# An encoder trunk on one core: the way from the output projection into the channel mixer, with the third tile turned inside the last projection and some sums on GpSimd

## The chip, the core and the metric

The kernel runs on one core of a Trainium2 chip. Its engines are TensorE (PE, with its weight loads as PEld), VectorE (DVE), ScalarE (ACT), GpSimd (POOL) and SyncE (SP), which issues most of the DMAs. Each engine works through its own list of instructions in a fixed order and waits on semaphores for the others. The metric is the device time of one execution in microseconds (us); lower is better.

## What is computed

Two requests, of 256 and 512 rows of width 1024 in f32, go through two layers with the same parameters. Each layer is a token mixer followed by a SwiGLU channel mixer, both between two RMS norms and added to the residual.

```python
def trunk(x, ...):
    for i in range(DEPTH):                          # 2 layers
        h = rms_norm(x, norm_mix_pre[i])
        m = window_gqa_sink(h, ...) if i % 2 == 0 else diff_attention(h, ...)   # end in "o @ w_o"
        x = x + rms_norm(m, norm_mix_post[i])
        h = rms_norm(x, norm_ffn_pre[i])
        x = x + rms_norm(swiglu(h, ffn_w_gate_up[i], ffn_w_down[i]), norm_ffn_post[i])
    return x

def swiglu(h, w_gate_up, w_down):
    g, u = jnp.split(h @ w_gate_up, 2, axis=-1)
    return (jax.nn.silu(g) * u) @ w_down
```

## The kernel before

The 768 rows are six tiles of 128, tiles 0 to 2 and 3 to 5. Every matrix product is made from three products of fp32r operands: a value is split into a high part (`hi`, a cast on ACT) and a low part (`lo`, value minus `hi`, on DVE), and hi·hi, hi·lo and lo·hi are added in PSUM (`product_steps`). The weights come from DRAM by SP's queue into a few buffers (`wraw`, `y_wraw`), are split by `two_parts` into `whi` and `wlo`, and a buffer's next load is issued once its low part has been made. `prepare` and `free` set how far this runs ahead.

The products of the channel mixer are made by a scheme that saves one of eight block products, on rows (tiles 0 to 2 against 3 to 5) and on halves of the columns. It needs combinations of both operands. For the activations, `combine` makes them: for a tile t < 3 it turns the tile on PE (`transpose`) and keeps `hhi`, `hlo` and a plain copy (`oa` in the first layer, `ob` in the second). For t >= 3 it turns the tile and makes s1, s2, s3 and a12 - s2 with the copy of tile t - 3, each split in two parts (`s1hi`, `s1lo` and so on). For the weights, `prepare` makes four combinations in place ("t32": L286 to L289, `b22` being split at L250 and L251), and the two pieces "t32" and "t14" are then split.

The stretch in question lies between the two, once in each layer. `project` multiplies the attention's result by the output weights; `staged` goes through the second half of the columns (`po_1`) in the order of tiles 0, 3, 1, 2, 4, 5, and between two half units of products it places the stages of the earlier tiles that `finish` returns: stage_a is 1/rms of the projection (`rstd_post`: an addition on ACT, a power on POOL), stage_b adds the residual (`x`), stores it and makes 1/rms of x (`rstd_pre`), stage_c scales x by it (`y_po`) and stage_d turns and combines it. The last five stages (two of tile 4, three of tile 5) are left over and become `later` in `ffn`, which places them among the first products of the channel mixer: p1 makes chunk c's px from a11 (tiles 0 to 2, left half) and copies it to `sv`, p2 adds the product with a12 and applies Silu (`ga`), p4 makes pz from a22, p6 and p5 make py and pw from s2 and s1. `u[0]` and `u[1]` are weight units of the first chunks.

The code's order is not yet the engines' order: a scheduler places each instruction when the kernel is built, by its dependences, by `high_priority` and by `issue_after`, which keeps the marked instructions behind another one. After that the order of each engine is fixed.

Of the kernel before, what the change touches and what calls it, by code (L numbers as in the profile page):

```python
# [17 lines left out]
P = 128  # L18
# [49 lines left out]
def trunk(  # L68
# [143 lines left out]
    ffn_units(1)  # L212

    raws, parts, b22s = {}, {}, {}
    state = {"dma": 0, "split": 0, "used": 0, "w": 0, "y": 0, "tt": 0, "rb": 0}
    tpool, dpool = [None], [None]
    quarters = {"tt": [], "rb": []}

# [29 lines left out]

    def two_parts(hi, lo, src):
        state["raw_hi"] = nc.scalar.copy(out=hi, in_=src)  # L250
        state["raw_lo"] = nc.vector.tensor_tensor(out=lo, in0=src, in1=hi.bitcast(F32), op=ALU.subtract)  # L251

    def prepare(upto):

# [75 lines left out]
    def split(hi, lo, src):  # L330
        state["hi"] = nc.scalar.copy(out=hi, in_=src)  # L331
        state["lo"] = nc.vector.tensor_tensor(out=lo, in0=src, in1=hi.bitcast(F32), op=ALU.subtract)  # L332

    def product_steps(out, pairs, start=True, stop=True, more=False):

        last = len(pairs) - 1

        def step(i):
            (ah, al), (bh, bl) = pairs[i]
            nc.tensor.matmul(out, ah, bh, start=start and i == 0, stop=False, skip_group_check=more)  # L343
            nc.tensor.matmul(out, ah, bl, start=False, stop=False, skip_group_check=more)  # L344
            nc.tensor.matmul(out, al, bh, start=False, stop=stop and i == last, skip_group_check=more)  # L345

        return [lambda i=i: step(i) for i in range(len(pairs))]

# [41 lines left out]

    def row_rstd(src, junk, name):
        ss = small.tile([P, 1], F32, tag="ss", name=f"ss_{name}")
        nc.scalar.activation(out=junk, in_=src, func=AF.Square, scale=D ** -0.5, accum_out=ss)
        return rstd(ss, eps_sb[:, 0:1], name)

    def scaled(y, src, r, g):
# [51 lines left out]
    def combine(src, t, name, comb, o):  # L448

        at = (t % 3) * P

        def turn(b):
            tp = bank(f"tp_{name}_{b}")
            for j in range(4):
                k = 4 * b + j  # L460
                nc.tensor.transpose(tp[:, j * P:(j + 1) * P], src[:, k * P:(k + 1) * P], ident)
            return tp

        v4 = lambda v: v.rearrange("p (k n) -> p k n", k=4)
        into = lambda half, b: tuple(v[half][:, 4 * b:4 * b + 4, at:at + P] for v in (h_hi, h_lo))
        if t < 3:
            for b in range(2):
                tp = turn(b)
                split(*into(0, b), v4(tp))
                nc.scalar.copy(out=o[t][:, b * 512:(b + 1) * 512], in_=tp)  # L470
            return
        a11, a12 = o[t - 3][:, :512], o[t - 3][:, 512:]
        s1, a22, s3, s2 = o[t][:, :512], o[t][:, 512:], src[:, :512], src[:, 512:]
        tp1, tp0 = turn(1), turn(0)
        nc.scalar.copy(out=a22, in_=tp1)
        split(*into(1, 1), v4(tp1))
        nc.vector.tensor_tensor(out=s1, in0=tp0, in1=a22, op=ALU.add)
        nc.vector.tensor_tensor(out=s3, in0=tp0, in1=a11, op=ALU.subtract)
        nc.vector.tensor_tensor(out=s2, in0=s1, in1=a11, op=ALU.subtract)
        split(*(v[:, :, at:at + P] for v in comb["s2"]), v4(s2))  # L480
        split(*into(1, 0), v4(s3))
        split(*(v[:, :, at:at + P] for v in comb["s1"]), v4(s1))
        nc.vector.tensor_tensor(out=a12, in0=a12, in1=s2, op=ALU.subtract)
        split(*(v[:, :, at:at + P] for v in comb["s4"]), v4(a12))

    def finish(sub, t, o, ssy, x, g, comb):

        r = {}
        m, (ss, y) = o[t], ssy

        def stage_a():
            with tc.high_priority():
                r[0] = rstd(ss[:, 1:2], ss[:, 0:1], f"post{sub}_{t}")

        def stage_b():
            with tc.high_priority():
                state["add"] = nc.vector.scalar_tensor_tensor(  # L500
                    out=x, in0=m, scalar=r[0], in1=x, op0=ALU.mult, op1=ALU.add)
                if g is not None:
                    r[1] = row_rstd(x, y, f"pre{sub + 1}_{t}")
            nc.sync.dma_start(out=x_at[sub + 1][t], in_=x)

        def stage_c():
            with tc.high_priority():
                scaled(y, x, r[1], g)

        def stage_d():  # L510
            if comb is not None:
                combine(y, t, f"h{sub + 1}_{t}", comb, o)
                return
            for s in transposes(y, t, f"h{sub + 1}_{t}"):
                s()

        return [stage_a, stage_b] + ([stage_c, stage_d] if g is not None else [])
# [9 lines left out]
    def staged(sub, units, o, sq, g, comb=None):  # L527

        st = []
        for i, t in enumerate((0, 3, 1, 2, 4, 5) if comb is not None else range(NT)):
            x = load_x(sub, t)
            units[t][0]()
            if i >= 2 and g is not None:
                st[i - 2][2]()
            if i >= 1:
                st[i - 1][1]()
            units[t][1]()  # L540
            if i >= 2 and g is not None:
                st[i - 2][3]()
            if g is None and t == NT - 1:
                last_tile(sub, t, o[t], sq[t], x, sq["last"])
                break
            st.append(finish(sub, t, o, sq[t], x, g, comb))
            st[i][0]()
        if g is None:
            return []
        return [st[NT - 2][2], st[NT - 1][1], st[NT - 2][3], st[NT - 1][2], st[NT - 1][3]]  # L550
# [18 lines left out]
    def out_unit(t, wk, o, n2, gp, sq, name):  # L569

        pm = bank(name)
        steps = product_steps(pm, [(htile(t, k), wk[k]) for k in range(KT)])
        if t == NT - 1:
            steps = releasing(steps, 4)
        return steps + [lambda: project_end(t, pm, o, n2, gp, sq, name)]

    def project_end(t, pm, o, n2, gp, sq, name):  # L580
            if n2 == 0:
# [443 lines left out]
    def ffn(layer, later, comb, cpool, cstack, ostack, gains):  # L1025
# [22 lines left out]
        def p1(c, unit):  # L1048
            mul(X, c, "px", "a11", unit, 0)
            sv[c] = temp("sv", c, AHEAD + 1, cpool)  # L1050
            nc.scalar.copy(out=sv[c], in_=X[c])

        def p2(c, unit):
            mul(X, c, "px", "a12", unit, 1, True)
            ga[c] = temp("ga", c, AHEAD + 1, cpool)
            nc.scalar.activation(out=ga[c], in_=X.pop(c), func=AF.Silu)

        def p6(c, unit):
            mul(Y, c, "py", "s2", unit, 1)
# [95 lines left out]


        c4, b5, d4, c5, d5 = later
        c4(), b5()
        u = take(2)
        p1(0, u[0]), p1(1, u[1])  # L1160
        d4()
        p2(0, u[0]), free(1), p2(1, u[1]), free(0)
        c5()
        u = take(2)
        p1(2, u[0]), p1(3, u[1])
        d5()
        p2(2, u[0]), free(1)
        ostack.close()
        tpool.append(steps.enter_context(tc.tile_pool(name=f"steps{layer}", bufs=1, reuse_waits="tile")))
# [404 lines left out]
```

## Time and profile before

| | |
|---|---|
| median of 3 runs | 1656.42 us (1656.40 to 1659.10) |
| profiled execution | 1656.38 us, span 1654.4 us, mean clock of TensorE 0.997 |
| busy in the span | PE 1618.3 us, DVE 1222.8, ACT 934.4, POOL 170.7 |
| first way from `po_1` to the mixer | px starts at 293.03 us, pz at 314.68 us |
| second | px starts at 1158.99 us |

A row of the timeline has the start and the duration in us, then engine, line, operation, the tile written and those read, partitions by elements, and in brackets how long the engine stood idle before it and what released it. A row of the waits has the engine and what waited, what it waited for, and the total in us, the times and the longest. A row of the stages has the window, its length, busy us of PE, PEld, DVE, ACT and POOL with the number of instructions in brackets, the granted clock of TensorE (PEclk), the share of the DMA engines and GB/s. Line numbers are those of the kernel before.

### The profile page before, as it was taken

What the parts mean: (1) busy time and instruction counts of PE and PEld (TensorE: products, weight loads), DVE (VectorE), ACT (ScalarE), POOL (GpSimd) and SP (SyncE); (2) the same over time, 40 slices, a digit from 0 to 9 for tenths busy, and PEclk for the clock granted to TensorE, in tenths of its full rate; (3) what the DMA queues carried; (4) which work ended last, traced back from release to release, by engine and by line L of the source; (5) the groups of instructions that cost most, each with busy time, mean ns of one, the idle gap of its engine ahead of it and who ended that gap; (6) DMA issues with size and microseconds to landing.
All of it is one profiled execution on the core that took longest, in us unless ns stands there. A gap on an engine that the chain in (4) does not pass through costs nothing. (4 is left out here: it accounts for less than half of the span.)

```text
span 1654.4 us, 24784 instructions
## 1 busy us (share of the span) xinstructions
PE 1618.3 (98%) x9163; PEld 1499.3 (91%) x9163; DVE 1222.8 (74%) x2167; ACT 934.4 (56%) x2038; POOL 170.7 (10%) x275
## 2 busy tenths in 40 slices
PE   7999999899999999999999999999899999999997
PEld 7888878899999998888999999888899999998886
DVE  7787756896766666888685886847896776656985
ACT  6777765654444444556475676766554444444553
POOL 1000001000000000001340461421000000000010
PEclk9999999999999999999999999999999999999999
DMA  6111104544333337675542332504443332337664
GB/s 217 40 39 49 37 16 153 178 137 139 101 131 110 131 116 246 239 253 180 156 111 69 98 84 79 152 1 166 153 156 123 117 125 97 131 129 254 228 238 159
DMA packets 70233, 220.64 MB, mean 133 GB/s; under 512 B 9249, under 2 KB 15521, under 8 KB 69857
## 3 DMA queue, kind: packets, MB, share of 16 engines
q1 hardware_dynamic: 54576, 175.93, 31.5%
q0 software_dynamic: 15392, 42.87, 9.1%
q8 instruction: 72, 1.18, 0.3%
q14 instruction: 49, 0.39, 0.1%
q10 hardware_dynamic: 144, 0.26, 0.0%
HBM read 163.59 MB, written 42.86 MB: 125 GB/s over the span
## 5 line engine op out<-in xcount | busy, mean ns | idle before, releaser
L251 DVE TENSOR_TENSOR wlo<-wraw,whi 128x1024 fp32r<-128x1024 f32 (+2 forms) x174 | 203.1, 1172 | 184.1 <-ACT whi L250 183.2
L250 ACT CAST whi<-wraw 128x1024 fp32r<-128x1024 f32 (+2 forms) x174 | 175.9, 1013 | 124.3 <-PE py L344 59.3
L343 PE MATMUL py<-hhi,whi 128*128 128x384 f32 x464 | 155.2, 335 | 0.3 <-ACT u L1061 0.3
L345 PE MATMUL py<-hhi,wlo 128*128 128x384 f32 x464 | 155.0, 334 | 0.0
L344 PE MATMUL py<-hlo,whi 128*128 128x384 f32 x464 | 155.0, 334 | 0.0
L331 ACT CAST hhi<-araw 128x768 fp32r<-128x768 f32 (+1 forms) x74 | 57.6, 782 | 91.3 <-DMA araw<-act 84.7
L343 PE MATMUL pv<-whi,hhi 128*128 128x512 f32 (+1 forms) x240 | 92.3, 385 | 0.0
L345 PE MATMUL pv<-whi,hlo 128*128 128x512 f32 (+1 forms) x240 | 92.2, 384 | 0.0
L344 PE MATMUL pv<-wlo,hhi 128*128 128x512 f32 (+1 forms) x240 | 92.1, 384 | 0.0
L332 DVE TENSOR_TENSOR hlo<-araw,hhi 128x768 fp32r<-128x768 f32 (+1 forms) x74 | 65.3, 889 | 32.6 <-ACT hhi L331 32.2
L343 PEld LDWEIGHTS py<-hhi,whi 128*128 128x128 f32 x464 | 87.1, 188 | 0.8 <-ACT u L1061 0.6
L344 PEld LDWEIGHTS py<-hlo,whi 128*128 128x128 f32 x464 | 87.1, 188 | 0.0
L345 PEld LDWEIGHTS py<-hhi,wlo 128*128 128x128 f32 x464 | 87.1, 188 | 0.0
L1114 POOL DMA_DIRECT2D act<-st x22 | 19.4, 882 | 636.6 <-DVE st L1113 636.6
L343 PE MATMUL po<-whi,hhi 128*128 128x512 f32 x192 | 78.4, 408 | 0.6 <-ACT hhi L331 0.6
L388 POOL TENSOR_TENSOR rstd_post<-rstd_post,mhalf 128x1 f32<-128x1 f32 x23 | 20.3, 885 | 544.9 <-ACT rstd_post L387 544.9
L345 PE MATMUL po<-whi,hlo 128*128 128x512 f32 x192 | 75.4, 393 | 0.9 <-DVE hlo L332 0.9
L901 ACT ACTIVATE be<-bsc,bmx 128x512 f32<-128x512 f32 (+1 forms) x96 | 58.7, 615 | 30.6 <-DVE bmx L899 30.0
L344 PE MATMUL po<-wlo,hhi 128*128 128x512 f32 x192 | 75.2, 392 | 0.0
L343 PE MATMUL px<-hhi,whi 128*128 128x384 f32 x208 | 69.8, 337 | 3.8 <-ACT hhi L331 2.8
L344 PE MATMUL px<-hlo,whi 128*128 128x384 f32 x208 | 69.7, 335 | 2.1 <-DVE hlo L332 2.1
L343 PE MATMUL pqa<-whi,hhi 128*128 128x384 f32 x192 | 71.1, 370 | 0.0
(307 smaller groups left out, 5049.0 us busy)
## 6 DMA issues: line engine op xcount, KB each, us to landing
act<-st POOLq DMA_DIRECT2D x22, 1344.0 KB, 6.6
wraw<-in_wgu SPq DMA_DIRECT2D x56, 512.0 KB, 4.7
araw<-act SPq DMA_DIRECT2D x70, 384.0 KB, 4.0
y_wraw<-in_wgu SPq DMA_DIRECT2D x40, 512.0 KB, 3.6
wraw<-in_wd SPq DMA_DIRECT2D x40, 512.0 KB, 4.0
xd<-x SPq DMA_DIRECT2D x18, 512.0 KB, 3.0
x<-xd SPq DMA_DIRECT2D x18, 512.0 KB, 4.3
wraw<-in_wo SPq DMA_DIRECT2D x16, 512.0 KB, 3.5
```

The source lines that it names most:

```text
L250: state["raw_hi"] = nc.scalar.copy(out=hi, in_=src)
L251: state["raw_lo"] = nc.vector.tensor_tensor(out=lo, in0=src, in1=hi.bitcast(F32), op=ALU.subtract)
L331: state["hi"] = nc.scalar.copy(out=hi, in_=src)
L332: state["lo"] = nc.vector.tensor_tensor(out=lo, in0=src, in1=hi.bitcast(F32), op=ALU.subtract)
L343: nc.tensor.matmul(out, ah, bh, start=start and i == 0, stop=False, skip_group_check=more)
L344: nc.tensor.matmul(out, ah, bl, start=False, stop=False, skip_group_check=more)
L345: nc.tensor.matmul(out, al, bh, start=False, stop=stop and i == last, skip_group_check=more)
L388: nc.gpsimd.tensor_tensor(out=r[:, :w], in0=r[:, :w], in1=mhalf[:, :w], op=ALU.pow)
L901: nc.scalar.activation(out=e[:, :n * P], in_=s, func=AF.Exp, bias=mx, accum_out=den[:, c:c + 1])
L1114: nc.gpsimd.dma_start(out=at_hand[c // 4][:, :, c // 2 % 2], in_=out.pop(c // 2))
```

## The change

- `turn` in `combine` places the four transposes of each bank behind the last product that was recorded (`state["mm"]`), and in `staged` the stage_d of tile 2 (the third tile of the first three) is recorded ahead of the second half of the last tile's products, so that its turn lies inside `po_1` of tile 5.
- In `combine`, a12 - s2 and the low part of s4 go from DVE to GpSimd; the high part stays on ACT.
- While the first half of the last tile's projection is recorded (`aside`), `two_parts` makes the low parts of two weight pieces on GpSimd, in halves of 512 columns.
- The square of `row_rstd` in stage_b of tile 4 is placed behind the last high part of the third tile (`behind`). The end of the last tile's projection and the combination of tile 5 get high priority, and so do the copies `sv` and `ga` on ACT.
- In `ffn` the later stages get other places: tile 4's stage_c behind the low part of tile 2, tile 5's stage_c ahead of p2 of chunk 0, the turn of tile 4 behind p2 of chunk 0, and the turn of tile 5 behind p1 of chunk 2.

```diff
     def two_parts(hi, lo, src):
         state["raw_hi"] = nc.scalar.copy(out=hi, in_=src)
-        state["raw_lo"] = nc.vector.tensor_tensor(out=lo, in0=src, in1=hi.bitcast(F32), op=ALU.subtract)
+        if not state["aside"]:
+            state["raw_lo"] = nc.vector.tensor_tensor(out=lo, in0=src, in1=hi.bitcast(F32), op=ALU.subtract)
+            return
+        for c in (slice(0, 512), slice(512, 1024)):
+            nc.gpsimd.tensor_tensor(out=lo[:, c], in0=src[:, c], in1=hi[:, c].bitcast(F32), op=ALU.subtract)
...
-            nc.tensor.matmul(out, al, bh, start=False, stop=stop and i == last, skip_group_check=more)
+            state["mm"] = nc.tensor.matmul(out, al, bh, start=False, stop=stop and i == last, skip_group_check=more)
...
-        nc.scalar.activation(out=junk, in_=src, func=AF.Square, scale=D ** -0.5, accum_out=ss)
+        with tc.issue_after(state["behind"].ins) if state["behind"] else ExitStack():
+            nc.scalar.activation(out=junk, in_=src, func=AF.Square, scale=D ** -0.5, accum_out=ss)
...
-            for j in range(4):
-                k = 4 * b + j
-                nc.tensor.transpose(tp[:, j * P:(j + 1) * P], src[:, k * P:(k + 1) * P], ident)
+            with tc.issue_after(state["mm"].ins):
+                for j in range(4):
+                    k = 4 * b + j
+                    nc.tensor.transpose(tp[:, j * P:(j + 1) * P], src[:, k * P:(k + 1) * P], ident)
...
-        nc.vector.tensor_tensor(out=a12, in0=a12, in1=s2, op=ALU.subtract)
-        split(*(v[:, :, at:at + P] for v in comb["s4"]), v4(a12))
+        nc.gpsimd.tensor_tensor(out=a12, in0=a12, in1=s2, op=ALU.subtract)
+        s4hi, s4lo = (v[:, :, at:at + P] for v in comb["s4"])
+        nc.scalar.copy(out=s4hi, in_=v4(a12))
+        nc.gpsimd.tensor_tensor(out=s4lo, in0=v4(a12), in1=s4hi.bitcast(F32), op=ALU.subtract)
...
-                combine(y, t, f"h{sub + 1}_{t}", comb, o)
+                with tc.high_priority() if t == NT - 1 else ExitStack():
+                    combine(y, t, f"h{sub + 1}_{t}", comb, o)
...
+            state["aside"] = i == NT - 1 and comb is not None
             units[t][0]()
+            state["aside"] = False
             if i >= 2 and g is not None:
                 st[i - 2][2]()
+                if i == NT - 1:
+                    st[i - 2][3]()
+                    state["behind"] = state["hi"]
             if i >= 1:
                 st[i - 1][1]()
+            state["behind"] = None
             units[t][1]()
-            if i >= 2 and g is not None:
+            if 2 <= i < NT - 1 and g is not None:
                 st[i - 2][3]()
...
-        return steps + [lambda: project_end(t, pm, o, n2, gp, sq, name)]
+
+        def end():
+            with tc.high_priority() if t == NT - 1 and n2 else ExitStack():
+                project_end(t, pm, o, n2, gp, sq, name)
+
+        return steps + [end]
...
             sv[c] = temp("sv", c, AHEAD + 1, cpool)
-            nc.scalar.copy(out=sv[c], in_=X[c])
+            with tc.high_priority():
+                nc.scalar.copy(out=sv[c], in_=X[c])
...
-            nc.scalar.activation(out=ga[c], in_=X.pop(c), func=AF.Silu)
+            with tc.high_priority():
+                nc.scalar.activation(out=ga[c], in_=X.pop(c), func=AF.Silu)
...
         c4, b5, d4, c5, d5 = later
-        c4(), b5()
+        with tc.issue_after(state["lo"].ins):
+            c4()
+        b5()
         u = take(2)
         p1(0, u[0]), p1(1, u[1])
+        c5()
+        p2(0, u[0]), free(1)
         d4()
-        p2(0, u[0]), free(1), p2(1, u[1]), free(0)
-        c5()
+        p2(1, u[1]), free(0)
         u = take(2)
-        p1(2, u[0]), p1(3, u[1])
+        p1(2, u[0])
         d5()
+        p1(3, u[1])
         p2(2, u[0]), free(1)
```

What this does to the order is shown at three places of the first layer; the second layer's are the same. In a tile's name the middle numbers are the projection's half and the tile (`y_po_1_4` is tile 4), the last one tells one buffer's use from another.

POOL, from the norm of tile 2 to that of tile 5, before:

```order
L388 TENSOR_TENSOR rstd_pre_2_3611<-rstd_pre_2_3611,mhalf 128x1
L388 TENSOR_TENSOR rstd_post_4_3646<-rstd_post_4_3646,mhalf 128x1
L388 TENSOR_TENSOR rstd_pre_4_3680<-rstd_pre_4_3680,mhalf 128x1
L388 TENSOR_TENSOR rstd_post_5_3732<-rstd_post_5_3732,mhalf 128x1
L388 TENSOR_TENSOR rstd_pre_5_3745<-rstd_pre_5_3745,mhalf 128x1
```

POOL in the same place, after:

```order
L392 TENSOR_TENSOR rstd_pre_2_3611<-rstd_pre_2_3611,mhalf 128x1
L489 TENSOR_TENSOR oa_229<-oa_229,y_po_1_3_3463 128x512
L492 TENSOR_TENSOR s4lo_3336<-oa_229,s4hi_3335 128x4x128
L392 TENSOR_TENSOR rstd_post_4_3646<-rstd_post_4_3646,mhalf 128x1
L255 TENSOR_TENSOR wlo_3659<-wraw_3378,whi_3658 128x512 x2
L255 TENSOR_TENSOR wlo_3672<-wraw_3390,whi_3671 128x512 x2
L392 TENSOR_TENSOR rstd_pre_4_3698<-rstd_pre_4_3698,mhalf 128x1
L392 TENSOR_TENSOR rstd_post_5_3734<-rstd_post_5_3734,mhalf 128x1
L392 TENSOR_TENSOR rstd_pre_5_3747<-rstd_pre_5_3747,mhalf 128x1
L489 TENSOR_TENSOR oa_230<-oa_230,y_po_1_4_3627 128x512
L492 TENSOR_TENSOR s4lo_3336<-oa_230,s4hi_3335 128x4x128
L489 TENSOR_TENSOR oa_231<-oa_231,y_po_1_5_3731 128x512
```

The sums and the halves of the weights' low parts have come among the powers of the norms (one more low part of s4 follows the last row).

DVE, where the first chunk's weights are combined, before (`wraw` are the two buffers of the chunk, `b` its quarter b22):

```order
L286 TENSOR_TENSOR wraw_3674<-wraw_3694,wraw_3674 128x512
L251 TENSOR_TENSOR b_3704<-wraw_3694,b_3704 128x512
L287 TENSOR_TENSOR wraw_3694<-wraw_3694 128x512
L479 TENSOR_TENSOR y_po_1_4_3627<-oa_233,oa_230 128x512
L288 TENSOR_TENSOR wraw_3694<-wraw_3694,wraw_3674 128x512
L332 TENSOR_TENSOR hlo_113<-y_po_1_4_3627,hhi_111 128x4x128
L289 TENSOR_TENSOR wraw_3674<-wraw_3674,wraw_3694 128x512
```

DVE in the same place, after (three rows stand ahead of these: L290, the first combination, L484 of tile 4, and L252 for `b`):

```order
L291 TENSOR_TENSOR wraw_3712<-wraw_3712 128x512
L485 TENSOR_TENSOR y_po_1_4_3627<-oa_233,oa_230 128x512
L483 TENSOR_TENSOR oa_234<-tp_h_5_0_3874,oa_234 128x512
L336 TENSOR_TENSOR hlo_113<-tp_h_5_1_3869,hhi_111 128x4x128
L484 TENSOR_TENSOR y_po_1_5_3731<-tp_h_5_0_3874,oa_231 128x512
L485 TENSOR_TENSOR y_po_1_5_3731<-oa_234,oa_231 128x512
L336 TENSOR_TENSOR s1lo_3332<-oa_234,s1hi_3331 128x4x128
L336 TENSOR_TENSOR hlo_113<-y_po_1_5_3731,hhi_111 128x4x128
L336 TENSOR_TENSOR s2lo_3334<-y_po_1_5_3731,s2hi_3333 128x4x128
L292 TENSOR_TENSOR wraw_3712<-wraw_3712,wraw_3676 128x512
L336 TENSOR_TENSOR s2lo_3334<-y_po_1_4_3627,s2hi_3333 128x4x128
L293 TENSOR_TENSOR wraw_3676<-wraw_3676,wraw_3712 128x512
```

Seven rows from the first combination to the last have become fifteen; the combination of tile 5 stands among them.

PE, at the start of the mixer, before (each px row has two more products of its kind behind it in the code):

```order
L461 MATMUL tp_h_2_1_3724<-ident,y_po_1_2_3561 128x128 x4
L343 MATMUL px_0_3749<-hhi_110,whi_3386 128x384
L343 MATMUL px_1_3764<-hhi_110,whi_3658 128x384
L461 MATMUL tp_h_4_1_3779<-ident,y_po_1_4_3627 128x128 x4
L461 MATMUL tp_h_4_0_3784<-ident,y_po_1_4_3627 128x128 x4
```

After, the turn of tile 2 (tp_h_2) stands behind twelve of the 24 products of `po_1` of tile 5, and the last product of the projection is followed by px alone:

```order
L349 MATMUL po_1_5_3651<-whi_3374,hlo_113 128x512
L347 MATMUL px_0_3751<-hhi_110,whi_3386 128x384
L348 MATMUL px_0_3751<-hlo_112,whi_3386 128x384
L349 MATMUL px_0_3751<-hhi_110,wlo_3387 128x384
L347 MATMUL px_0_3751<-hhi_110,whi_3386 128x384
```

The turn of tile 4 now has 36 products of px ahead of it, that of tile 5 24 more; pz, which uses the last combined piece, comes behind 96.

More of the change, by code (lines that the diff above doesn't have):

```diff
@@ L214, in trunk @@
     raws, parts, b22s = {}, {}, {}
-    state = {"dma": 0, "split": 0, "used": 0, "w": 0, "y": 0, "tt": 0, "rb": 0}
+    state = {"dma": 0, "split": 0, "used": 0, "w": 0, "y": 0, "tt": 0, "rb": 0, "aside": False, "behind": None}
     tpool, dpool = [None], [None]
```

## The prediction

> **What bounds the kernel now.** I read the page first, then PE's waits, then the two stretches in which PE waits for the pieces that the change moves, engine by engine.
>
> ```profile
> span 1654.4 us, 24784 instructions
> PE 1618.3 (98%) x9163; PEld 1499.3 (91%) x9163; DVE 1222.8 (74%) x2167; ACT 934.4 (56%) x2038; POOL 170.7 (10%) x275
> ```
>
> PE is the bound: a change pays only where PE stands still. The profiled execution took 1656.38 us, 2.0 us around its span, and stands 0.04 us from the median of the runs (1656.42), so the sum is made against 1656.4. Under 0.2% (3.3 us) a measurement of this kernel cannot tell from no change. PE's waits from 268 to 340 us (the way into the first channel mixer, seven rows), and from 1135 to 1215 us (into the second, four rows):
>
> ```profile
> PE px L343 <- ACT hhi L331: 1.4, 1, 1.4
> PE px L344 <- DVE hlo L332: 1.1, 1, 1.1
> PE px L343 <- ACT sv L1051: 1.0, 1, 1.0
> PE py L344 <- DVE s2lo L332: 0.9, 1, 0.9
> PE pz L343 <- ACT whi L250: 0.8, 1, 0.8
> PE tp_h L461 <- DVE y_po L397: 0.3, 1, 0.3
> PE py L343 <- ACT u L1061: 0.3, 1, 0.3
> ...
> PE py L344 <- DVE s2lo L332: 2.2, 1, 2.2
> PE px L343 <- ACT hhi L331: 1.5, 1, 1.5
> PE px L344 <- DVE hlo L332: 1.1, 1, 1.1
> PE tp_h L461 <- DVE y_po L397: 0.3, 1, 0.3
> ```
>
> They add up to 5.8 and 5.1 us. The second place has lost more: after the wait of 2.2 us the granted clock falls. One row of the windows by stage (the sixth figure group is PEclk), then PE's rows there and in the first place:
>
> ```profile
> 1186.00:1189.40 3.40, 3.40 (x12) 3.40 (x13) 3.40 (x5) 2.51 (x3) 0.00 (x0) 0.57 0.33 86
> ...
> 1187.38 0.52 PE L343 MATMUL py<-s2hi,whi 128*128 128x384 f32 x1
> 1187.70 0.52 PE L344 MATMUL py<-s2lo,whi 128*128 128x384 f32 x1
> ...
> 293.03 0.62 PE L343 MATMUL px<-hhi,whi 128*128 128x384 f32 x2 [1.38 <-ACT hhi L331]
> 308.36 1.04 PE L461 MATMUL tp_h<-ident,y_po 128*128 128x128 f32 x8
> 313.30 0.33 PE L344 MATMUL px<-hlo,whi 128*128 128x384 f32 x1
> 314.68 0.33 PE L343 MATMUL pz<-hhi,whi 128*128 128x384 f32 x1
> ```
>
> Starts stand 0.32 us apart. In the first place eight follow from 313.30 to 314.68, 0.173 apart. Over 3.4 us that is half a clock, 1.7 us lost. So 5.8 + 6.8 = 12.6 us is all that the change can win, 0.8%.
>
> The Trainium skill (TensorE: Matmul & The Clock Gate, Part 1) has the array fall to half its clock after an idle window of about 3.4 us. By that rule a wait of 2.2 us would cost itself alone; the trace disagrees, since the row above stands behind 2.2 us.
>
> **The change, part by part.** Both places get the same new order, so I work the first and carry it over.
>
> *Sums on GpSimd.* Ten instructions of 512 columns leave DVE for POOL at each place: the a12 sum and the s4 low part for three tiles, and the low parts of two weight pieces in halves. DVE is relieved of eight instructions. What they cost on POOL, and what they do to DVE, is shown where POOL works on tiles of that size:
>
> ```profile
> 956.42 1.05 POOL L963 TENSOR_TENSOR ob<-ob,rstd_sub 128x512 f32<-128x512 f32 x1
> 961.39 1.64 POOL L963 TENSOR_TENSOR ob<-ob,rstd_sub 128x512 f32<-128x512 f32 x1
> 961.18 0.95 DVE L251 TENSOR_TENSOR wlo<-wraw,whi 128x768 fp32r<-128x768 f32 x1
> 962.05 1.40 DVE L836 TENSOR_TENSOR zq<-xq,rope 128x384 f32<-128x384 f32 x1
> 968.24 0.55 DVE L836 TENSOR_TENSOR zk<-xk,rope 128x384 f32<-128x384 f32 x1
> 1084.98 0.83 POOL L963 TENSOR_TENSOR ob<-ob,rstd_sub 128x384 f32<-128x384 f32 x1
> 1084.75 0.61 DVE L925 SCALAR_TENSOR_TENSOR hlo<-tp_o,subl,hhi 128x384 fp32r<-128x384 f32 x1
> ```
>
> A sum takes 1.05 us alone. The one at 961.39 began inside a DVE instruction on two SBUF tiles and took 1.64; the next DVE instruction, also on two SBUF tiles, then ended at 963.45 where 0.55 us was due: it stood still until POOL was done at 963.03. The instruction at 1084.75, which reads one tile from PSUM, was not held. So the two engines take turns wherever DVE reads two SBUF tiles. Each sum either waits for DVE or holds it for up to 1.05 us. Bounds: 0 to 1.05 us of DVE for each.
>
> *What queues behind them on POOL.* In the new order the sums stand among the powers that make each tile's norm. Before, those stood here, with what they released on DVE, SP and ACT:
>
> ```profile
> 283.16 0.55 POOL L388 TENSOR_TENSOR rstd_pre<-rstd_pre,mhalf 128x1 f32<-128x1 f32 x1 [3.03 <-ACT rstd_pre L387]
> 292.00 0.57 POOL L388 TENSOR_TENSOR rstd_pre<-rstd_pre,mhalf 128x1 f32<-128x1 f32 x1 [4.15 <-ACT rstd_pre L387]
> 293.25 1.05 POOL L388 TENSOR_TENSOR rstd_post<-rstd_post,mhalf 128x1 f32<-128x1 f32 x1 [0.68 <-ACT rstd_post L387]
> 296.14 1.28 DVE L500 SCALAR_TENSOR_TENSOR x<-oa,rstd_post,x 128x1024 f32<-128x1024 f32 x1
> 297.34 1.22 DVE L251 TENSOR_TENSOR wlo<-wraw,whi 128x1024 fp32r<-128x1024 f32 x1
> 298.58 0.33 SPq L224 DMA_DIRECT2D wraw<-in_wgu  x1
> 304.23 0.69 DVE L286 TENSOR_TENSOR wraw<-wraw,wraw 128x512 f32<-128x512 f32 x1 [1.92 <-DMA wraw<-in_wgu]
> 307.90 0.69 DVE L289 TENSOR_TENSOR wraw<-wraw,wraw 128x512 f32<-128x512 f32 x1
> 308.91 1.04 ACT L250 CAST whi<-wraw 128x1024 fp32r<-128x1024 f32 x1
> ...
> 1164.54 0.33 SPq L224 DMA_DIRECT2D wraw<-in_wgu  x1
> 1168.92 0.69 DVE L286 TENSOR_TENSOR wraw<-wraw,wraw 128x512 f32<-128x512 f32 x1 [0.66 <-DMA wraw<-in_wgu]
> ```
>
> From 283.7, POOL now has two sums (2 x 1.05 us, a wait of 1.2 behind a 1.28 us instruction of DVE, and 0.7 for ACT's cast between them), a power of 1.0, four halves (4.2, and 1.2 behind tile 4's x) and two powers (1.6): 295.7. It also waits for ACT, whose weight casts and squares come behind copies of held tiles: bounds 0 and 4 us, I take 2. So rstd_post of tile 5 is there at about 297.7 where it was at 294.3. Tile 5's x runs to 299, the third low part of the weights to 300.3, at worst 301.5, and only then may SP issue the load that waits for its buffer, at about 301 instead of 298.58. Such a load released DVE 5.65 us after its issue here and 4.4 at the second place: 305.4 or 306.7 for the first combination of the weights (L286, now L290). I take 305.7, nearer the shorter, since the load of a gain that shared the queues then is further back.
>
> *The order on DVE.* From L286 to L289 seven instructions stand 0.6 apart, 304.23 to 308.6. Now tile 5's combination has priority, and 15 stand there: 15 x 0.6 = 9.0 us. Four of POOL's sums fall into the same stretch, beside eleven instructions on two SBUF tiles; I take three holds, 3.1 us (bounds 0 and 4.2), since one sum starts beside PSUM-fed ones. L293 ends at 305.7 + 9.0 + 3.1 = 317.8. ACT's cast of this piece (1.04, as at 308.91) releases pz at 318.9.
>
> *When PE gets there.* The third tile's turn inside the last projection keeps PE busy, but its casts stand on ACT behind a weight cast and a copy that waits for a held DVE: I keep 1.2 of the 1.4 us at px's first product, 0.6 of the 1.1 for hlo. The turn of tile 4 now has 36 products (6.2 us) ahead of it, so its norm (rstd_pre at 292.00 now, behind the four halves at about 297) is covered; without them that would be a wait of 4 us. The copy of sv stays behind a weight cast whose load is released by POOL: 1.0 stays, and 0.2 at px's fourth group. PE starts px at about 293.1, has 96 products (16.6), two turns (2.1) and 1.8 of these waits: 313.6, against 314.68 now. There it stands for 318.9 - 313.6 = 5.3 us. Behind that the clock halves: 1.7.
>
> *After that.* The wait for s2lo goes, since s2lo is made ahead of L293. L293 comes 9.2 us later than L289 did (308.6), PE about 7 (5.3 + 1.7): the two waits of 1.1 in all for whi and u, which hang on the next weight pairs, grow by up to 2; I take 1.6 together.
>
> The sum at each place: 1.2 + 0.6 + 1.0 + 0.2 + 5.3 + 1.7 + 1.6 = 11.6 us lost, against 5.8 and 6.8 now: +5.8 and +4.8, together +10.6. No other stretch changes its order, and PE at 98% has no slack behind that gives it back: 1656.4 + 10.6 = 1667.0. Priority for sv and ga is costed at nothing: ACT was idle 44% of the span, and the copy waits for its load, not its turn. SP's x of tile 4 and 5 now go ahead of weight loads, inside the bounds of the landing (4.3 to 5.65).
>
> **Rivals.** *The sums miss each other.* If POOL's sums fall beside PSUM-fed DVE instructions, L293 ends at 314.7 and pz waits about 2.2 us. For it: four of the 15 instructions read PSUM. Against: the sums are released by just the instructions that stand in front of the contending ones. Loss 3.0 + 2.2 + 1.6 = 6.8 without the half clock, 8.5 with it: 1657.4 or, as the row at 1186 has it, 1660.8. By the page's rule it would be the first of these.
>
> *Faster.* If the holds are gone in the earlier stretch too (POOL through by 295, the load issued at about 298.5), L293 ends by about 313, pz waits under 1 us and the clock stays. It decides at a wait of 2 us before pz. Loss 3.0 + 0.8 + 1.6 = 5.4, and 2.4 where the third tile's casts also come before px: 1654.6 down to 1648.6, 1651 between. Against it: DVE's order is fixed, and 15 instructions must run behind the load.
>
> *Longer.* Five holds and a load of 5.65 us at both places: +3 at each, 1674.
>
> **How the numbers follow.** Forecast 0.58, the sums miss 0.17, faster 0.20, longer 0.05. The forecast alone spans 1661 to 1672 (two to four holds, the two landings); from 1651 to 1674 the range takes in the misses and half of the faster case. Faster by over 0.2%: 0.18. Within: 0.14, the cheaper misses and the weakest of the faster case. Slower: 0.58 + 0.05 + 0.05 = 0.68.
>
> **What would show it.** In the profile after: a wait of PE at pz's first product for whi, 4 to 7 us, at both places, a PEclk near 0.5 for 3.4 us behind it; POOL's sums at 1.05 to 2.2 us, DVE instructions on two SBUF tiles at 1.6 to 1.7 where 0.68 stood; s2lo out of PE's waits. I am wrong if DVE's rows there keep 0.68, if L293 ends before PE finishes px, or if PE's wait moves to the turns of tiles 4 and 5.

## The result: about 9 us slower, and the profile after

The changed kernel takes 1666.2 us in the median (1664.69 to 1668.92, six runs) against 1657.3 for the kernel before in the same comparison (1656.4 to 1659.1): a ratio of 1.0055, with a 95% interval of 1.0044 to 1.0065. The prediction was 1667.0, in a range of 1651 to 1674. The profiled execution's span grew from 1654.4 to 1664.7 us. Three of the kernels below had one execution each far off (2224 to 5707 us), which the medians here leave out, so that a kernel which later expectations have at 1658.7 stands at 1658.6.

From the page of the changed kernel:

```profile
span 1664.7 us, 24769 instructions
PE 1620.2 (97%) x9163; PEld 1500.8 (90%) x9163; DVE 1223.7 (74%) x2151; ACT 933.7 (56%) x2038; POOL 195.3 (12%) x295
```

PE's work is the same and DVE is no freer than before (1223.7 us busy against 1222.8, with 16 instructions fewer): what was taken from it came back as longer instructions. POOL has 24.6 us more. PE's waits in the two stretches, 268 to 350 and 1135 to 1225 us:

```profile
PE pz L347 <- ACT whi L250: 5.9, 2, 5.1
PE px L347 <- ACT sv L1072: 1.7, 2, 1.2
PE px L348 <- DVE hlo L336: 1.0, 1, 1.0
PE px L347 <- ACT hhi L335: 0.6, 1, 0.6
...
PE pz L347 <- ACT whi L250: 5.9, 2, 5.1
PE px L347 <- ACT sv L1072: 2.0, 3, 1.3
PE px L348 <- DVE hlo L336: 1.0, 1, 1.0
PE px L347 <- ACT hhi L335: 0.5, 1, 0.5
```

The wait for s2lo is gone, and a wait of 5.1 us for the weight piece `whi` at pz's first product stands in its place, at both ways into the mixer. The sums of the waits are 9.2 and 9.4 us, where 5.8 and 5.1 stood. What makes it late, from the timeline of the first place, engine by engine:

```profile
301.78 0.33 SPq L224 DMA_DIRECT2D wraw<-in_wgu  x1
...
307.03 0.69 DVE L290 TENSOR_TENSOR wraw<-wraw,wraw 128x512 f32<-128x512 f32 x1 [1.06 <-DMA wraw<-in_wgu]
...
310.64 0.68 DVE L336 TENSOR_TENSOR hlo<-tp_h,hhi 128x512 fp32r<-128x512 f32 x1
...
312.70 1.50 DVE L336 TENSOR_TENSOR s1lo<-oa,s1hi 128x512 fp32r<-128x512 f32 x1 [0.18 <-ACT s1hi L335]
314.12 1.77 DVE L336 TENSOR_TENSOR hlo<-y_po,hhi 128x512 fp32r<-128x512 f32 x1
...
316.42 1.74 DVE L292 TENSOR_TENSOR wraw<-wraw,wraw 128x512 f32<-128x512 f32 x1
...
318.69 0.68 DVE L293 TENSOR_TENSOR wraw<-wraw,wraw 128x512 f32<-128x512 f32 x1
...
310.20 1.30 POOL L489 TENSOR_TENSOR oa<-oa,y_po 128x512 f32<-128x512 f32 x1 [7.21 <-DVE y_po L485]
312.23 1.43 POOL L492 TENSOR_TENSOR s4lo<-oa,s4hi 128x512 fp32r<-128x512 f32 x1 [0.73 <-ACT s4hi L491]
313.61 1.74 POOL L489 TENSOR_TENSOR oa<-oa,y_po 128x512 f32<-128x512 f32 x1
316.08 1.54 POOL L492 TENSOR_TENSOR s4lo<-oa,s4hi 128x512 fp32r<-128x512 f32 x1 [0.73 <-ACT s4hi L491]
...
319.53 1.04 ACT L250 CAST whi<-wraw 128x1024 fp32r<-128x1024 f32 x1
...
315.14 0.34 PE L349 MATMUL px<-hhi,wlo 128*128 128x384 f32 x1
320.62 0.69 PE L347 MATMUL pz<-hhi,whi 128*128 128x384 f32 x1 [5.14 <-ACT whi L250]
```

From L290's start to L293's end DVE takes 12.34 us for 15 instructions. Three of them are longer than the 0.68 us of their neighbours, by 0.82, 1.09 and 1.06 us: 2.97 together. Each of the three reads two SBUF tiles and runs beside one of POOL's sums, and each of the three sums is longer than 1.05 us as well: the two engines stand in each other's way. The sum at 310.20 runs beside rows that read one tile from PSUM (`tp_h`, as at 310.64), and none of these is held.

### The profile page after: what moved, and what is told of

It reads as the page before. It is cut to its first block, busy times and chain, and to the rows that moved or that the text cites. A ratio compares the mean times of both kernels' runs of the same rounds, so it can differ in the third digit from the quotient of the medians.

```text
span 1664.7 us, 24769 instructions
## 1 busy us (share of the span) xinstructions
PE 1620.2 (97%) x9163; PEld 1500.8 (90%) x9163; DVE 1223.7 (74%) x2151; ACT 933.7 (56%) x2038; POOL 195.3 (12%) x295
## 5 line engine op out<-in xcount | busy, mean ns | idle before, releaser
L252 DVE TENSOR_TENSOR wlo<-wraw,whi 128x1024 fp32r<-128x1024 f32 (+1 forms) x170 | 198.0, 1170 | 183.2 <-ACT whi L250 182.5
L392 POOL TENSOR_TENSOR rstd_post<-rstd_post,mhalf 128x1 f32<-128x1 f32 x23 | 14.9, 650 | 541.5 <-ACT rstd_post L391 541.5
```

Of the source, the lines that this page charges most:

```text
L392: nc.gpsimd.tensor_tensor(out=r[:, :w], in0=r[:, :w], in1=mhalf[:, :w], op=ALU.pow)
```

## Experiments

The theory to begin with (A) is the prediction's: pz waits because L293 ends late, behind a load that POOL's chain delays, behind 15 rows, and behind three holds by POOL's sums; the half clock behind the wait is lost as well. Its rivals: the order alone (B), the late load alone (C); later the clock (D), an interaction with the new order (E), and holds alone (H). The kernel before took 1656.9 us beside the first and the third group of these runs and 1657.5 beside the second; a ratio is to that, with its 95% interval in brackets.

**All sums back on DVE.** `state["aside"]` is never set, and

```diff
-        nc.gpsimd.tensor_tensor(out=a12, in0=a12, in1=s2, op=ALU.subtract)
-        s4hi, s4lo = (v[:, :, at:at + P] for v in comb["s4"])
-        nc.scalar.copy(out=s4hi, in_=v4(a12))
-        nc.gpsimd.tensor_tensor(out=s4lo, in0=v4(a12), in1=s4hi.bitcast(F32), op=ALU.subtract)
+        nc.vector.tensor_tensor(out=a12, in0=a12, in1=s2, op=ALU.subtract)
+        split(*(v[:, :, at:at + P] for v in comb["s4"]), v4(a12))
```

> The changed kernel with all ten sums of each place back on DVE (the a12 sum, the s4 low part, the low parts of the two weight pieces); its order on PE, the third tile's early turn and the priorities stay. Theory A (holds and a late load): of the 12.3 us that DVE takes from L290's start to L293's end in the changed kernel, 9.4 are 15 rows and 3.0 are three holds; here 17 rows without holds, 10.8. POOL has only the norms left, and the load is issued between 299 and 301 instead of 301.8. Together 1.5 to 4.3 us less at each place, and half of the clock's 2 us where pz's wait falls under 2: 1659, from 1656 to 1663; pz still waits 1 to 3.5 us. Theory B (the order alone, the 15 rows ahead of L293): two rows more, 1.2 us at each place: 1668. Theory C (the load alone, late behind POOL): the holds do not matter, 1661, and the kernel with the halves alone back on DVE gives the same.

1657.7 us, ratio 1.0001 [0.9993, 1.0010]: the whole loss is gone. Theory A's range held it; B's 1668 did not come. The new order, the third tile's early turn and the priorities together cost and bring nothing that can be measured. PE still waits for whi at pz (2.6 us at the first product, at both ways): such a wait is no loss by itself, since others that the kernel before had are gone.

**Only the a12 sums and s4 low parts back on DVE** (the diff above, without the change to `aside`).

> The changed kernel with the a12 sums and the s4 low parts back on DVE; the low parts of the two weight pieces stay on POOL in halves. Theory A: the three holds (3.0 us) leave DVE's stretch, two rows (1.2) come in, and the two sums ahead of tile 4's norm leave POOL (2.1 us and their waits), so that the load comes 0 to 3 us sooner: 1.8 to 4.8 us less at each place, 1660, from 1656 to 1663. Theory B (order alone): 1668. Theory C (load alone): the halves are the longer part of POOL's delay (6.0 of 8.8 us) and stay, so this gives less than the kernel with the halves back on DVE: about 1664.

1658.6 us, 1.0012 [1.0003, 1.0021]: as A has it, and against B and C. Two rows of DVE's timeline in this kernel, the first and the last of the 17 instructions:

```profile
305.30 0.69 DVE L290 TENSOR_TENSOR wraw<-wraw,wraw 128x512 f32<-128x512 f32 x1 [2.24 <-DMA wraw<-in_wgu]
...
314.92 0.68 DVE L293 TENSOR_TENSOR wraw<-wraw,wraw 128x512 f32<-128x512 f32 x1
```

10.30 us for 17 instructions, none longer than 0.69, against 12.34 for 15 with the holds. PE waits 4.3 us for whi at pz here, 0.8 less than in the changed kernel, and 5.7 us in all at each way, against 9.2 and 9.4.

**Only the halves of the two weight pieces back on DVE** (`aside` never set, the other sums stay on POOL).

> The changed kernel with the low parts of the two weight pieces back on DVE (2 x 1.2 us); the a12 sums and s4 low parts stay on POOL. Theory A: the three holds and the 15 rows stay; the load is up to 2 us sooner behind POOL, less up to 1.2 us for the two instructions on DVE: 1664, from 1661 to 1667, and DVE's rows of 1.5 to 1.8 us between L290 and L293 are still there. Theory B: no change, 1666. Theory C (load alone): POOL's 6 us leave the chain, the load is issued near 299, at least 2.5 us less at each place: 1659 to 1661.

1668.3 us, 1.0070 [1.0055, 1.0086]: 1.3 us above A's range, and C falls. The halves are no part of the loss. If anything they help beside the other sums (2.1 us, with intervals that overlap), and without them they make 0.9 (1658.6 against 1657.7). In the profile px's wait for hlo is 2.0 us instead of 1.0, and pz still waits 4.8 and 5.1.

**The last tile's combination without priority**: the `with tc.high_priority()` in stage_d taken out.

> The changed kernel without the priority for the last tile's combination: L292 and L293 then stand ahead of tile 5's eight rows on DVE. Theory A: L293 ends behind 7 rows and a hold at about 312.5, pz does not wait any more for whi (5.1 us and the clock's 2 saved), but the eight rows of tile 5 and two holds come behind it, s2lo is ready near 320 where PE is there at 317.5, and the pieces of the next pair come later too: the wait moves to py's s2lo and pz's next group, 0 to 2 us less at each place: 1664, from 1661 to 1667. Theory B (order alone is the loss): back to the kernel before, 1656 to 1658.

1666.0 us, 1.0056 [1.0044, 1.0068]. Now 8 rows stand from L290 to L293, they take 6.0 us with one hold among them (1.79 us at 310.89; the next, 1.75 us, is on the row behind L293), and pz no longer waits for its first whi; yet the time is that of the changed kernel. The order alone (B) is ruled out a second time: the waits go to hlo (1.8), the next whi (1.0), `st` and s2lo. They add up to 6.4 and 7.2 us only, 5 us less than in the changed kernel. What takes this back in the profile is the clock: half-clock stretches start at 295.6, 319.5, 1073.8 and 1186.5 us, and half of PE's busy time within them is 8.1 us, against 4.0 in the changed kernel.

**PE kept at work through its wait.** Ahead of pz's real products of chunk 0:

```diff
...
+                for _ in range(28):
+                    nc.tensor.matmul(Z[c], k0[:, :P], k0, start=True, stop=True, skip_group_check=True)
...
```

`k0` is a block of hhi. 

> The changed kernel with 28 products of 128x384 (0.173 us each, 4.9 us) written into pz's own bank ahead of its real products, which overwrite them: PE works through its wait for whi. In the order, pz's twelve products now stand together ahead of py's, where before they were mixed. Theory A (the half clock is a loss of its own): no half clock behind the wait, 2.1 us less at each place: 1662. Theory D (the slow products only cover what is late next): pz's third product needs the low part of the same piece, which ends 1.6 us behind whi (322.24 against 320.57 in the changed kernel), so that about 1.3 of the 2.1 come back as a wait for wlo: 1664.6 or more. If the clock has no part in it: 1666.

1668.9 us, 1.0069 [1.0056, 1.0082]: no gain. No half clock stands in its records in either stretch, but PE's waits from 268 to 350 us now read, among others:

```profile
PE pz L347 <- ACT whi L250: 1.4, 2, 1.0
...
PE pz L349 <- DVE wlo L252: 1.1, 1, 1.1
```

Waits of 6.1 us and 4.9 us of added products make 11.0, against the changed kernel's 9.2 of waits and 1.9 of slow products. By this account the half clock was no loss of its own there: products at full speed reach the next late piece sooner and wait for it. The time alone fits D as well as a clock without any part in it; the new waits speak for D, with the reservation that pz's products stood in another order. Why it is 2.7 us slower than the changed kernel, with intervals that overlap, is open.

**The sums alone, in the kernel before**: there only the four lines of the first diff go the other way.

> The kernel before with one part of the change: the a12 sums and the s4 low parts on POOL (six of the ten sums of each place); the order of turns, the halves and the priorities stay as before. Theory A (the sums cost by holds and by POOL's chain wherever they stand): the two sums ahead of tile 4's norm come with 2.1 us and waits on POOL, the load is 1 to 3 us later, and one to three holds lengthen the rows from L286 to the s2 low part: py's wait for s2lo grows by 2 to 4 us at each place and the clock falls behind it: 1665, from 1661 to 1669. Rival E (the sums hurt only in the new order, where 15 rows stand in front of L293): 1656 to 1659, with py's wait for s2lo unchanged.

1666.3 us, 1.0055 [1.0043, 1.0067]: a loss as large as the whole change's, without any of the new order. E falls. PE's waits on the first way, then on the second (first rows of each):

```profile
PE py L344 <- DVE s2lo L332: 3.5, 1, 3.5
PE px L343 <- ACT hhi L331: 2.9, 1, 2.9
...
PE py L344 <- DVE s2lo L332: 3.5, 1, 3.5
PE px L343 <- ACT hhi L331: 2.8, 1, 2.8
```

They were 0.9 and 1.4, 2.2 and 1.5. All waits of the two ways are up by 4.9 us (7.9 each, from 5.8 and 5.1); half-clock stretches are five between 20 and 1200 us, where the kernel before has two, and half of PE's busy time in all of them is 8.3 us, from 3.3. So about half of the loss comes as slow products. Which tile's sums do it in the old order was not tried.

**Which of the sums?** In the changed kernel, `eng = nc.gpsimd if t == 3 else nc.vector` and, the other way about, `t > 3`. Tile 3's two sums stand ahead of tile 4's norm on POOL, those of tiles 4 and 5 behind all norms, beside the rows from L290 to L293.

> The changed kernel with only tile 3's a12 sum and s4 low part on POOL, where they stand ahead of tile 4's norm; those of tiles 4 and 5 are back on DVE (17 rows from L290 to L293, no hold among them). The kernel with all three tiles' sums back on DVE took 1658.7, the changed one 1666.2: 7.5 us, 3.75 at each place. Theory A (two prices): POOL's chain. The norms of tiles 4 and 5 come later by the two sums, PE's last projections and the load with them, 1.9 us by the shift of L290 against the start of the projections (53.5 to 55.3 us behind it): 1662.5, from 1660.5 to 1664.5. Theory H (holds alone): 1658.7. Theory C (POOL's chain alone): 1666.

> The changed kernel with tile 3's a12 sum and s4 low part back on DVE, those of tiles 4 and 5 on POOL, behind all norms (15 rows from L290 to L293 and the three holds). Theory A (two prices): the holds, 3.0 us, less two rows on DVE, 1.0 to 1.2: 1.9 us at each place more than 1658.7: 1662.5, from 1660 to 1664.5, with L290 to L293 at 12.3 us. Theory H (holds alone): 1666. Theory C (POOL's chain alone): 1658.

Tile 3's alone: 1661.1, 1.0023 [1.0012, 1.0035]. Tiles 4 and 5's alone: 1667.5, 1.0065 [1.0052, 1.0077]. Against 1658.6 with none of them these are 2.5 and 8.9 us, and 7.6 with all. So the two prices do not add up: the sums of tiles 4 and 5 are enough for the whole loss, as H has it, where A had given each half. What the 2.5 us of tile 3's are is not shown: in its profile the waits of the two ways are 6.2 and 4.8 us, together no more than the 5.7 and 5.7 with none. With tiles 4 and 5's the stretch on DVE is again 12.34 us long, 2.0 more than without holds (10.30), and L290 itself starts 1.25 us later than there. The rows of this kernel, DVE's, ACT's and then PE's:

```profile
306.55 0.69 DVE L290 TENSOR_TENSOR wraw<-wraw,wraw 128x512 f32<-128x512 f32 x1 [2.80 <-DMA wraw<-in_wgu]
...
318.21 0.68 DVE L293 TENSOR_TENSOR wraw<-wraw,wraw 128x512 f32<-128x512 f32 x1
...
311.06 0.62 ACT L492 CAST s4hi<-oa 128x512 fp32r<-128x512 f32 x1 [0.69 <-POOL oa L490]
311.59 0.61 ACT L335 CAST s1hi<-oa 128x512 fp32r<-128x512 f32 x1
312.11 0.47 ACT L1073 COPY sv<-px 128x384 f32<-128x384 f32 x1
...
319.05 1.03 ACT L250 CAST whi<-wraw 128x1024 fp32r<-128x1024 f32 x1
...
312.63 0.45 PE L347 MATMUL px<-hhi,whi 128*128 128x384 f32 x1 [1.34 <-ACT sv L1073]
...
320.14 0.69 PE L347 MATMUL pz<-hhi,whi 128*128 128x384 f32 x1 [5.13 <-ACT whi L250]
```

The cast of s4hi waits for POOL's sum, the copy that PE needs stands behind it on ACT, and PE stands still for 1.3 us. This stop does not add to the loss ahead of pz: pz starts when whi is cast, behind L293 on DVE, and a PE that had come 1.3 us sooner would have waited there so much longer. The waits of the two kernels from 268 to 350 us, with all sums of this kind on DVE and then with those of tiles 4 and 5 on POOL:

```profile
PE pz L347 <- ACT whi L250: 4.3, 1, 4.3
PE px L348 <- DVE hlo L336: 1.4, 1, 1.4
...
PE pz L347 <- ACT whi L250: 5.9, 2, 5.1
PE px L347 <- ACT sv L1073: 2.0, 2, 1.3
PE px L348 <- DVE hlo L336: 1.3, 1, 1.3
```

3.5 us more here and, by the same view, 2.9 on the second way (5.7 to 8.6): 6.4 of the 8.9. The rest is not accounted for; executions of one kernel differ by as much (1657.6 to 1660.9 us with all sums of this kind on DVE). How much of the 3.5 us the holds make and how much the later start of L290 was not separated.

**The third tile's early turn alone, in the kernel before** (the changes to `turn`, `row_rstd` and `staged`, without `aside`).

> The kernel before with one part of the change: the third tile's turn inside the last projection, and the turns ordered behind the last product written ahead of them; no sums on POOL, no new priorities, the later turns as before. If the earlier turn pays by itself, PE's waits for hhi and hlo at px (1.4 and 1.1 us at each place) go: 1653 to 1655. Theory A: the third tile's casts wait on ACT and DVE behind the copies for the projection's end, the wait is one for hlo of 2 to 4 us in place of the two: 1657 to 1660.

1660.7 us, 1.0018 [1.0009, 1.0027], just above what A had. PE's wait at px on the first way is one for hlo:

```profile
PE px L348 <- DVE hlo L336: 3.7, 1, 3.7
```

It stands in place of 1.4 and 1.1 us. By itself the early turn costs; among the other parts of the change, as in the run with all sums on DVE, no such cost is left over.

**The priority alone, cut down, in the kernel before**: in `combine`, everything from the turns to the split of s1 under

```diff
+        with tc.high_priority() if t == NT - 1 else ExitStack():
```

so that only a12 - s2 and the split of s4 keep their place.

> The kernel before with one part of the change, cut down: priority for the last tile's combination without its a12 sum and s4 low part. On DVE the s2 low part and the rest of tile 5 then stand ahead of the low part of the next weight piece. py's wait for s2lo (0.9 and 2.2 us, the second with 1.7 of half clock) goes, pz's next group waits up to 1.3 for the later low part: 2 to 4 us less: 1654.5, from 1653 to 1657. Rival (DVE's work is the same, so the wait changes its name): 1657 to 1659.

1651.1 us (1650.49 to 1653.31), 0.9966 [0.9954, 0.9979]: faster than both kernels, and below the expected range. The reason stands in DVE's rows on the second way, before and in this kernel:

```profile
1183.23 0.69 DVE L286 TENSOR_TENSOR wraw<-wraw,wraw 128x512 f32<-128x512 f32 x1 [1.67 <-DMA wraw<-in_wgu]
...
1185.25 0.68 DVE L332 TENSOR_TENSOR s2lo<-y_po,s2hi 128x512 fp32r<-128x512 f32 x1
```

```profile
1175.99 0.68 DVE L332 TENSOR_TENSOR s2lo<-y_po,s2hi 128x512 fp32r<-128x512 f32 x1
...
1183.71 0.69 DVE L286 TENSOR_TENSOR wraw<-wraw,wraw 128x512 f32<-128x512 f32 x1 [0.72 <-DMA wraw<-in_wgu]
```

Before, the s2 low part that PE waits for stood behind L286 of the next weight pair, which waited for a load. Now it is done 7 us before that load is used. PE's waits from 1130 to 1230 us are down to 2.5 us (from 5.1), on the first way to 4.2 (from 5.8), and in this profile no half clock follows them or the wait at 1067 us, which had cost 1.7 us each; one fall stands at 1157.7 instead. The fall at 1067 us stands behind a wait that both kernels have, so its absence may be luck of this execution.

**Two other versions** brought nothing. The third tile's turn and the halves on POOL kept, a12 and s4 on DVE without priority, the later turns as before, no priority for the projection's end:

> The parts of the change that the runs so far leave standing: third tile's turn inside the last projection and the two weight pieces' low parts on POOL. The a12 sums and s4 low parts are back on DVE and keep no priority (two rows fewer ahead of the next weight piece), the rest of the last tile's combination keeps it; the turns of tiles 4 and 5 stand as in the kernel before; no priority for the last projection's end. Theory A: px's wait for hlo stays (1.4), pz's of 4.3 and the clock behind it go, the waits for s2lo and for the next whi of 0.5 to 1.5 each stay: about 4 us lost at each place against 5.8 and 6.8: 1653.5, from 1651 to 1656. Rival: DVE's work in the stretch is the same, the waits only change their names, 1657 to 1659.

1656.3 us, 0.9996 [0.9986, 1.0005]: no gain, and 5.2 us more than with the priority of tile 5's combination alone. What this version has beyond that (the early turn, the halves on POOL, the priority of `sv` and `ga`) takes its gain back; which of them was not tried. Its waits on the two ways are 3.7 and 4.6 us, 2.6 less than before, but of the stretch from 372 to 1040 us, where the kernel before has none that the view shows, it says, with two smaller ones behind it:

```profile
PE tp_h L440 <- DVE y_pd L402: 1.3, 1, 1.3
```

The same with 11 products of 128x512 in the turn's bank, ahead of the wait for `be` in the second mixer:

> The kernel with the best parts, and 11 products of 128x512 (0.227 us each, 2.5 us) in one more place, the second mixer, where PE stands 2.6 to 2.7 us for tile be ahead of a turn (1067 us in the kernel before) and the clock in the records fell for 3.4 us behind it in most runs' profiles. They write the turn's own bank ahead of it. Theory A: no half clock there, 1.7 us less than the same kernel without them where it fell: 0.5 to 1.7 us in the median. If the clock falls by a count of its own (phase) and not by the wait: no difference. If the products come later than the wait and lengthen it: up to 2.5 us more.

1658.0 us, 1.0004 [0.9994, 1.0013]: no gain. There is no half clock in that place in its profile, which is of the slowest of its twelve executions (1662.3 us), and a fall at 329.2, 1165.5 and 1199.6 us instead.

## Why the prediction was right, and where its parts were not

The time came within 1 us (against the kernel before, at 1657.3 us beside it, the change is 8.9 us where 10.6 was forecast), by the place and the mechanism it named: a wait for whi at pz, 5.3 us predicted and 5.14 measured, at both ways. The range says little, since 1651 to 1674 holds the time of the kernel before as well; what was borne out is the forecast with its wait. (The longer case, 3 us more at each place, makes 1673 and not the 1674 that ends the range.) The pieces:

- *The stretch from L290 to L293*: 9.0 and 3.1 us predicted, 9.37 and 2.97 measured. Three holds, as taken, on instructions with two SBUF tiles. The Trainium skill (SBUF — State Buffer, "SBUF: two separate sides") has DVE and GpSimd take turns on a shared port pair in such cases, each for its whole instruction. The trace agrees: holds of up to 1.09 us, and none on the rows between them that read PSUM.
- *The load and PE's arrival* were both placed too early, L290 by 1.3 us (305.7 against 307.03) and PE at pz by 1.7 (313.6 against 315.3). That the two errors cancel in the wait is luck.
- *px's waits*: hhi 1.2 predicted, 0.6 measured; hlo 0.6 and 1.0; sv 1.0 and 0.5. The fourth group's 0.2 was mis-sized most: 1.2 us, since ACT's cast of s4hi waits for POOL ahead of sv. It makes PE later at pz and the wait there shorter, so the total hardly feels it. The prediction asked what queues behind the sums on POOL, and not what queues behind those who wait for them.
- *The half clock*: 1.7 predicted; 12 products took 4.01 us from 320.62 instead of 2.08, 1.9. *Later waits*: 1.6 predicted, 0.8 measured (5.9 less 5.1). The two belong together, as the waits of the run with PE kept at work suggest.

The sum of the first place is 0.6 + 1.0 + 1.7 + 5.1 + 1.9 + 0.8 = 11.1 where 11.6 was predicted, of the second 11.3; against 5.8 and 6.8 this is 9.8 us, and the spans differ by 10.3. One term stands outside the two places: the kernel before has another half-clock stretch at 1067 us, 1.6 us of slow products, which the changed kernel lacks. With it 9.8 becomes 8.2, and about 2 us of the 10.3 have no place in this account; that the sum came so near the time is luck in part.

What the experiments take back is how the prediction shared the loss out. It charged 4.8 us at each place to eight more rows ahead of L293, and about 1.5 to a load made late by POOL. Neither is a price of its own: with all ten sums on DVE the same order, even longer by two rows, is as fast as before, presumably since those rows had to be done anyway and s2lo no longer waits; and with POOL's chain shortened but the holds kept (tiles 4 and 5) nothing is won. Nor does the named wait by itself tell a loss from none: 4.3 of its 5.1 us are still there with the sums back on DVE and the halves on POOL, at 1658.6 us, where the other waits are smaller. The rival "the sums miss each other" was priced at 1657.4 to 1660.8, and 1657.7 and 1658.6 is where the kernels without holds came out.

The step on the clock was right in size and wrong in its rule. It read the row at 1186 us as a half clock that any wait of 2.2 us brings. The windows below, whose columns are window, length, busy us of PE, PEld, DVE, ACT and POOL, the granted clock, the DMA share and GB/s, show two of the kernel before and then five of the changed one:

```profile
1183.05:1186.46 3.41, 1.17 (x7) 0.85 (x7) 3.12 (x6) 0.62 (x1) 0.00 (x0) 1.00 0.00 0
1186.46:1189.88 3.42, 3.42 (x12) 3.42 (x12) 3.42 (x6) 2.85 (x4) 0.00 (x0) 0.50 0.46 141
...
314.60:318.01 3.41, 0.88 (x6) 0.55 (x4) 3.41 (x3) 1.01 (x2) 2.29 (x2) 1.00 0.12 16
318.01:321.43 3.41, 0.81 (x2) 0.81 (x3) 3.41 (x6) 2.37 (x3) 0.00 (x0) 0.50 0.37 138
321.43:324.84 3.41, 3.41 (x12) 3.41 (x12) 1.42 (x2) 0.00 (x0) 0.00 (x0) 0.50 1.00 336
...
1068.95:1072.36 3.41, 2.32 (x11) 1.53 (x9) 3.32 (x8) 3.31 (x8) 1.87 (x3) 1.00 0.86 306
1072.36:1075.77 3.41, 1.88 (x15) 1.83 (x16) 3.36 (x8) 2.93 (x12) 1.51 (x2) 1.00 0.59 203
```

Each window here in which PE is busy for about 1.2 us or less is followed by one at half clock, from its first moment. The last two hold a wait of 2.62 us for `be`, ending at 1073.89; it is cut in two by the edge at 1072.36, and the clock stays. The Trainium skill (TensorE: Matmul & The Clock Gate, Part 1) has a free-running window of 3413 ns; the trace agrees, as the section on the hardware shows. It speaks of an idle window; here one in which PE is busy for a third of it (1.17 of 3.41 us) is enough.

## What to carry to other kernels

An engine that has time to spare is no free place for a sum: look which instructions of the other engine run beside it on the same port, and who stands behind the one that waits for its result. Look in each engine's line for an instruction that waits for a load ahead of a piece that the bounding engine needs soon; to move the piece ahead of it was worth 0.34% here, more than anything that was taken off the busy engine. And test the parts of a change one at a time, since their prices need not add up.

## What the runs showed of the hardware

- *The clock is judged on a fixed grid.* In each of the fourteen profiles, after the first 20 us, the half-clock stretches start whole multiples of 3.413 us from each other: in the kernel before at 1066.997 and 1186.464 us, 35.0 windows apart, in the changed one at 318.013 and 1188.412, 255.0 apart. Counted over PE's records in all of them, no window at full clock with more than 1.88 us of work was followed by half clock, every one with under 1.5 was, and between them both occur. So what a wait of 2 to 3 us costs depends on where it falls. The execution times of a kernel go with the clock: the five of the kernel with the halves back on DVE go from 1664.0 us at a mean clock of 0.995 to 1673.2 at 0.991.
- *An earlier load did not land earlier by as much.* With tiles 4 and 5's sums on POOL the load was issued at 299.25 us, 2.5 us sooner than in the changed kernel, and L290 started at 306.55, 0.5 sooner. What else bounds it was not tried.
